# A list-scheduled two-layer encoder step: the planner's estimate lets a VectorE instruction between SBUF tiles last until the GpSimd product beside it ends

## The chip, the cores and the metric

The kernel runs on one core of a Trainium2 chip. The metric is the device time of one execution in microseconds (us), shown as the median of several runs. The engines are called as the profile calls them: PE is TensorE (PEld its weight load), DVE is VectorE, ACT is ScalarE, POOL is GpSimd, SP is SyncE, which here issues the DMAs.

## What is computed

Two layers of a hybrid encoder on 1104 tokens (64 of a running stream, 16 meta tokens and 1024 of a new one), width 1024. Each layer is, cut to what matters here:

```python
h = rmsnorm(x, norm_g)
z = h @ w_in                       # one projection, its columns split among the groups below
y_a = bg * conv(cg * xin) * silu(ga)                                   # short gated convolution
y_b = attention(rmsnorm(cq) @ w_uq, rmsnorm(ckv), kr) * silu(gb)       # 8 heads, latent keys, rotary part kr
zs = zc + (prev - zc) * shift_mu                                       # token shift
y_c = groupnorm(rwkv7_scan(r, decay, k, v, kk, a, s0)) * silu(gc)      # recurrence over tokens, 4 heads
x = x + concat([y_a, y_b, y_c]) @ w_out
```

A last RMSNorm follows, and the states of every group are outputs too.

## The kernel before

Features lie on the partitions, tokens along the free axis, in three groups of 336, 384 and 384 tokens (`GROUPS`). A projection of 128 output columns for one group (`project`) is 24 matmuls into one PSUM tile `prj`: 8 slices of the 1024 inputs, and for each `whi` by `hhi`, `whi` by `hlo` and `wlo` by `hhi`, since weights and activations are split into a high and a low half. ACT makes the high half and DVE the low one (`halves`: `whi`, then `wlo`). The weights' halves live in a ring of slots, so that a new `whi` waits until PE has finished with an older one.

The recurrence is done in chunks of 64 tokens. For each of 6 parts (3 token groups by 2 pairs of heads) `rwkv_prep` makes triangular matrices (PSUM tiles `x`, masked by DVE into `wq` or `wx`), transposes (`tm`), inverts 16 by 16 blocks on DVE with a chain of tiny instructions on 48 partitions (`tri`, `lora`) between two trips through DRAM (`dg`, `dt`), and combines blocks on PE (`inv`). `rwkv_scan` then carries the state from chunk to chunk: a product `xp`, an addition on DVE (`wr`), a copy on ACT (`wx`), a product `sp`, and the new `state` on DVE. `rwkv_finish` takes a product `yp`, the group norm, a transpose `ym` and the gate. GpSimd takes products between SBUF tiles: the token shift (`zd`), norm factors (`xin`, `krt`, `cq`, `ckv`) and gates (`gate`, `qa`).

The order of the instructions is made when the program is written. Every operation goes through `Meter`, which keeps for each engine a time at which it comes free, for each tile the times of its last writes and reads, and gives each instruction a cost from its engine, operation and size (`note`). The main stream (the projections, `inproj_rest`) issues its matmuls one by one; after each, `pump` looks at the side streams (prep, scan, finish, attention's preparation), asks with `due` when what their next step needs will be ready by the estimate, and lets a step go in between when that is no later than PE's clock and a margin. So the estimate decides how many projection matmuls stand between two steps of the recurrence. The engines themselves take their instructions in the order in which they were issued, and semaphores make them wait for data.

`place` can put an instruction into an earlier gap of its engine in the estimate:

```python
for i, (a, b) in enumerate(idle):
    s = max(a, t)
    if s + cost <= b:
        ...
        return s
s = max(t, self.free[eng])
```

All instructions stand on one line of the profile (line 82, the call through which every operation is recorded), so groups are told apart by their tiles.

Of the kernel before, what the change touches and what calls it, by code (L numbers as in the profile page):

```python
# [55 lines left out]
COLUMNS = (*(11 + m for m in MIXED), 18, 19, 0, 1, 2, KR, *range(3, 11), *range(20, 24))  # L56
NEVER = 1e9
LEAD = 0.0
WARM = 8
NEAR = 0.0  # L60
LAZY = -1.3
# [10 lines left out]
class Engine:  # L72


    def __init__(self, meter, name, eng):
        self.meter, self.name, self.eng = meter, name, eng
# [12 lines left out]
class Meter:  # L89


    def __init__(self, nc):
        self.nc = nc
        self.free = dict.fromkeys(("tensor", "vector", "scalar", "gpsimd", "sync"), 0.0)
        self.seen, self.rings, self.part = {}, {}, (128, 128)
        self.idle = {e: [] for e in self.free}
        for e in self.free:
            setattr(self, e, Engine(self, e, getattr(nc, e)))

# [30 lines left out]
    def note(self, eng, op, args, kw):  # L130
        aps = [x for x in args + tuple(kw.values()) if isinstance(x, bass.AP)]
        if not aps:
            return
        outs = [kw["out"] if "out" in kw else args[0]] + ([kw["accum_out"]] if "accum_out" in kw else [])
        ins = [x for x in aps if not any(x is o for o in outs)]
        size = lambda x: int(np.prod(x.shape[1:]))
        n = max(size(x) for x in outs[:1] + ins)
        if eng == "tensor":
            l, r = args[1], args[2]
            p, q = (2, 1) if op == "transpose" else (4, 2) if l.dtype == F32 else (1, 1)  # L140
            l, r = (r, l) if op == "transpose" else (l, r)
            cost, late = max(size(r) * p, 2 * size(l) * q) / 2320, 0.0
            if l.dtype == F32 and size(l) <= 64 and op == "matmul":
                cost = 0.02 + size(r) * 2 / 2320
            cost += 0.003
            up = lambda x: 32 if x <= 32 else 64 if x <= 64 else 128
            part = (up(l.shape[0]), up(size(l))) if l.dtype == F32 and op == "matmul" else (128, 128)
            cost += CHANGE if part != self.part else 0.0
            self.part = part
        elif op == "dma_start":  # L150
            cost, late = 0.45, 2.0 + size(outs[0]) * outs[0].shape[0] * 4 / 2e5
        else:
            fast = op in ("tensor_copy", "tensor_scalar") and all(x.space == bass.MemoryType.SB for x in aps)
            cost, late = {"vector": 0.1 + n * 0.54e-3 if fast else 0.1 + n * 1.06e-3, "scalar": (0.37 if "accum_out" in kw else 0.18) + n * 0.83e-3,
                          "gpsimd": 0.15 + n * (0.7e-3 if op == "memset" else 2.1e-3 if op == "tensor_tensor" else 3.4e-3)}[eng], 0.0
        t = self.place(eng, max([self.when(x, eng) for x in ins] + [self.when(x, eng, True) for x in outs]), cost)
        for x in ins:
            self.touch(x, eng, t + cost + late, False)
        for x in outs:
            self.touch(x, eng, t + cost + late, True)  # L160
# [35 lines left out]
class Net:  # L196
# [86 lines left out]
    def race(self, streams, fill):  # L283
# [3 lines left out]
        while run:  # L287
            more = fill if self.solo else []
            t, q = next(((0.0, q) for q in run + more if self.due(q[0]) <= self.clock + LEAD), (NEVER, None))
            if q is None:  # L290
# [1101 lines left out]
    def run(self):  # L1392
# [16 lines left out]
        ps = self.psp("warm")  # L1409
        for _ in range(WARM):  # L1410
            self.mm(ps[:, :128], self.ones, self.ones, start=True, stop=True)
# [168 lines left out]
```

## Time and profile before

| what | value |
|---|---|
| median of 3 runs | 1530.34 us (1526.41 to 1530.67) |
| the profiled execution | 1529.08 us, span of its instructions 1527.0 us |
| PE busy | 1463.1 us, 96% of the span |
| DVE busy | 1063.0 us, 70% |
| ACT busy | 772.1 us, 51% |
| POOL busy | 253.1 us, 17% |
| mean granted TensorE clock | 0.988 |

A row of a timeline gives an instruction's start and duration in us, its engine, operation, tiles written and read, shapes and count, and in brackets how long its engine had been idle before it and what ended that. Matmuls overlap in their records, so their pace is read from start to start. A table by windows gives each engine's busy time in a stretch and the granted TensorE clock there, where 1.00 is 2.4 GHz and 0.50 is 1.2 GHz.

### The profile page before, as it was taken

What the parts mean: (1) busy time and instruction counts of PE and PEld (TensorE: products, weight loads), DVE (VectorE), ACT (ScalarE), POOL (GpSimd) and SP (SyncE); (2) the same over time, 40 slices, a digit from 0 to 9 for tenths busy, and PEclk for the clock granted to TensorE, in tenths of its full rate; (3) what the DMA queues carried; (4) which work ended last, traced back from release to release, by engine and by line L of the source; (5) the groups of instructions that cost most, each with busy time, mean ns of one, the idle gap of its engine ahead of it and who ended that gap; (6) DMA issues with size and microseconds to landing.
All of it is one profiled execution on the core that took longest, in us unless ns stands there. A gap on an engine that the chain in (4) does not pass through costs nothing.

```text
span 1527.0 us, 30583 instructions
## 1 busy us (share of the span) xinstructions
PE 1463.1 (96%) x12076; PEld 1310.9 (86%) x12076; DVE 1063.0 (70%) x2477; ACT 772.1 (51%) x1846; POOL 253.1 (17%) x281
## 2 busy tenths in 40 slices
PE   8999999999999999999999999999999999999996
PEld 7989988999887878779999898898998768788795
DVE  7565687676778676575845666876767877686566
ACT  7125454444567575563522355445356775565442
POOL 0222212222121101000011222212122301111002
PEclk9999999999999999999999999999999999999998
DMA  6322212322225101122322312212322331012123
GB/s 209 137 83 81 68 50 57 88 55 75 82 86 164 31 26 39 55 74 63 141 103 99 117 33 60 88 30 81 76 67 77 129 98 47 24 35 85 41 66 119
DMA packets 95471, 119.81 MB, mean 78 GB/s; under 512 B 41889, under 2 KB 74785, under 8 KB 95329
## 3 DMA queue, kind: packets, MB, share of 16 engines
q1 hardware_dynamic: 95328, 117.87, 25.4%
q8 instruction: 95, 1.56, 0.4%
q14 instruction: 48, 0.39, 0.1%
HBM read 81.24 MB, written 36.60 MB: 77 GB/s over the span
## 4 chain that ended last, share of the span: by engine, by line
PE 51%; DVE 10%; ACT 5%; issue 3%; DMA 2%; POOL 1%; DVEq 0%; SPq 0%; ACTq 0%; POOLq 0%
PE prj L82 24%; PE sc L82 6%; PE po L82 6%; PE tr L82 5%; PE upq L82 3%; PE val L82 1%; PE inv L82 1%; DVE st L82 1%; DVE p L82 1%; PE upk L82 1%; ACT p L82 1%; DVE wq L82 1%; DVE out L82 1%; ACT pt L82 1%; ACT wq L82 1%
## 5 line engine op out<-in xcount | busy, mean ns | idle before, releaser
L82 PE MATMUL prj<-hhi,whi 128*128 128x384 f32 (+1 forms) x1152 | 392.0, 340 | 4.2 <-DVE z L82 2.6
L82 PE MATMUL prj<-hlo,whi 128*128 128x384 f32 (+1 forms) x1152 | 391.9, 340 | 0.1
L82 PE MATMUL prj<-hhi,wlo 128*128 128x384 f32 (+1 forms) x1152 | 391.1, 339 | 0.7 <-DVE wlo L82 0.7
L82 PEld LDWEIGHTS prj<-hhi,whi 128*128 128x128 f32 x1152 | 219.7, 191 | 7.5 <-issue 2.9
L82 PEld LDWEIGHTS prj<-hlo,whi 128*128 128x128 f32 x1152 | 219.6, 191 | 4.1 <-issue 0.9
L82 PEld LDWEIGHTS prj<-hhi,wlo 128*128 128x128 f32 x1152 | 219.5, 191 | 4.0 <-DVE wlo L82 1.0
L82 PE MATMUL prj<-yhi,wo 128*128 128x384 f32 (+2 forms) x776 | 206.5, 337 | 2.5 <-DVE xn L82 2.0
L82 PE MATMUL sc<-ka,qa 128*128 128x264 f32 (+9 forms) x720 | 156.3, 337 | 6.0 <-ACT p L82 2.5
L82 ACT ACTIVATE p<-sc,st 128x144 f32<-128x144 f32 (+8 forms) x240 | 127.9, 541 | 42.4 <-DVE st L82 41.6
L82 PEld LDWEIGHTS prj<-yhi,wo 128*128 128x128 f32 x776 | 138.6, 189 | 5.1 <-DVE xn L82 3.1
L82 DVE TENSOR_REDUCE st<-sc 128x1 f32<-128x512 f32 (+9 forms) x240 | 118.1, 501 | 23.9 <-PE sc L82 22.3
L82 PE MATMUL prj<-ylo,wo 128*128 128x384 f32 (+2 forms) x388 | 129.6, 334 | 0.0
L82 PEld LDWEIGHTS sc<-ka,qa 128*128 128x128 f32 (+1 forms) x720 | 112.3, 188 | 18.8 <-ACT p L82 6.4
L82 ACT ACTIVATE pt<-tr 128x512 f32<-128x512 f32 (+3 forms) x174 | 92.4, 546 | 70.2 <-PE tr L82 68.2
L82 PE MATMUL tr<-cst,p 128*128 128x128 f32 (+2 forms) x752 | 115.5, 277 | 4.5 <-ACT pt L82 3.1
L82 PEld LDWEIGHTS tr<-cst,p 128*128 128x128 f32 (+2 forms) x752 | 83.2, 141 | 28.3 <-issue 10.3
L82 POOL TENSOR_TENSOR qa<-qt,qa 128x512 fp32r<-128x512 f32 (+1 forms) x40 | 49.7, 1244 | 338.6 <-ACT qa L82 338.5
L82 ACT ACTIVATE whi<-wraw 128x1024 fp32r<-128x1024 f32 (+1 forms) x49 | 51.0, 1041 | 97.4 <-PE prj L82 82.5
L82 PE MATMUL po<-pt,v 128*64 128x256 f32 (+3 forms) x864 | 94.3, 354 | 0.4 <-ACT pt L82 0.4
L82 DVE TENSOR_SCALAR p<-p,st 80x336 f32<-80x336 f32 (+5 forms) x144 | 84.2, 587 | 1.8
L82 DVE TENSOR_TENSOR wlo<-wraw,whi 128x1024 fp32r<-128x1024 f32 (+1 forms) x49 | 71.4, 1458 | 16.9 <-ACT whi L82 16.8
L82 PEld LDWEIGHTS po<-pt,v 128*64 128x64 f32 (+1 forms) x864 | 53.2, 137 | 27.4 <-issue 4.5
(232 smaller groups left out, 2641.9 us busy)
## 6 DMA issues: line engine op xcount, KB each, us to landing
wraw<-w_in SPq DMA_DIRECT2D x47, 512.0 KB, 3.6
wraw<-w_out SPq DMA_DIRECT2D x32, 256.0 KB, 2.6
zd<-z SPq DMA_DIRECT2D x14, 576.0 KB, 3.5
wr<-zd SPq DMA_DIRECT2D x36, 192.0 KB, 2.8
gd<-gate SPq DMA_DIRECT2D x12, 552.0 KB, 3.4
yraw<-yd SPq DMA_DIRECT2D x8, 552.0 KB, 3.8
xn<-x SPq DMA_DIRECT2D x8, 552.0 KB, 4.2
xd<-xn SPq DMA_DIRECT2D x8, 552.0 KB, 2.9
```

What stands on the lines that cost most here:

```text
L82: r = f(*args, **kw)
```

## The change

The estimate of an instruction's cost changes; what is computed does not. `Meter` now remembers the stretches in which it has placed GpSimd products (`busy`). A DVE instruction of four kinds, all of whose operands lie in SBUF and which has at most 512 elements per partition, and which would begin at DVE's frontier while such a product runs, is given a cost that reaches 0.1 us past the product's end.

```diff
+SHARES = ("tensor_tensor", "scalar_tensor_tensor", "tensor_copy", "tensor_scalar")
...
-        self.idle = {e: [] for e in self.free}
+        self.idle, self.busy = {e: [] for e in self.free}, []
...
-        t = self.place(eng, max([self.when(x, eng) for x in ins] + [self.when(x, eng, True) for x in outs]), cost)
+        ready = max([self.when(x, eng) for x in ins] + [self.when(x, eng, True) for x in outs])
+        if eng == "vector" and op in SHARES and n <= 512 and all(x.space == bass.MemoryType.SB for x in aps):
+
+            t = max(ready, self.free[eng])
+            cost = max([cost] + [b - t + 0.1 for a, b in self.busy if a < t + 0.1 < b])
+        t = self.place(eng, ready, cost)
+        if eng == "gpsimd" and op == "tensor_tensor":
+            self.busy = self.busy[-40:] + [(t, t + cost)]
```

The instructions stay the same but for six copies out of PSUM, which move from ACT to DVE. Their order changes from the first part of the recurrence on. In the rows below L82 of the kernel before is L83 of the changed one.

**Place A**, PE's order in the first part of layer 1, where the triangular products `x` end and the transposes `tm` begin (`prj` are projection matmuls). Before:

```order
L82 MATMUL x_128_963<-wb_884,wx_886 64x128
L82 MATMUL x_129_964<-wb_884,wx_886 64x128
L82 MATMUL prj_939<-hhi_158,wlo_791 128x336
L82 MATMUL prj_989<-hhi_151,whi_790 128x384
L82 MATMUL prj_989<-hlo_159,whi_790 128x384
L82 MATMUL prj_989<-hhi_151,wlo_791 128x384
L82 MATMUL prj_989<-hhi_152,whi_790 128x384
L82 MATMUL tm_994<-cst,wx_886 128x128 x3
L82 MATMUL prj_989<-hlo_160,whi_790 128x384
L82 MATMUL tm_999<-cst,wx_886 128x128 x3
```

The same place in the changed kernel, the end of it:

```order
L83 MATMUL prj_989<-hlo_166,whi_790 128x384
L83 MATMUL prj_989<-hhi_158,wlo_791 128x384
L83 MATMUL prj_1015<-hhi_151,whi_790 128x384
L83 MATMUL prj_1015<-hlo_159,whi_790 128x384
L83 MATMUL prj_1015<-hhi_151,wlo_791 128x384
L83 MATMUL prj_1015<-hhi_152,whi_790 128x384
L83 MATMUL prj_1015<-hlo_160,whi_790 128x384
L83 MATMUL tm_1021<-cst,wx_886 128x128 x3
L83 MATMUL tm_1026<-cst,wx_886 128x128 x3
```

Between the last `x` and the first `tm` there stood 5 projection matmuls, and now there stand 30. Layer 2 has the same counts.

**Place B**, DVE's order in the third part of the recurrence, beside the rotary keys (`kr`, `krt`) and the projection `xin`. `wr<-xp` is the scan's addition, for which ACT's `wx` and then PE's `sp` wait; `wq<-dg` and `wa<-dt` are the inverted blocks, for which PE's `inv` waits; `wlo` is the low half of the next weights. Before:

```order
L82 COPY tri_2207<-tri_2207 48x256
L82 TENSOR_TENSOR kr_2305<-kr_2305 32x384
L82 SCALAR_TENSOR_TENSOR kr_2305<-krt_2306,rot 32x384
L82 TENSOR_TENSOR wlo_2394<-wraw_2303,whi_2393 128x1024
L82 SCALAR_TENSOR_TENSOR krt_2306<-krt_2306,rot 32x384
L82 TENSOR_TENSOR wr_1412<-xp_2425,wq_1423 64x128
...
L82 TENSOR_TENSOR kr_2305<-kr_2305 32x384
L82 SCALAR_TENSOR_TENSOR state_140<-sp_2473,dc_1483,sd_2423 64x64 x2
L82 TENSOR_TENSOR wq_2054<-dg_2204,cst 128x6x64
L82 TENSOR_TENSOR wa_2053<-dt_2286,cst 128x384
L82 TENSOR_TENSOR wlo_2497<-wraw_2397,whi_2496 128x1024
```

Now:

```order
L83 TENSOR_TENSOR wlo_2394<-wraw_2270,whi_2393 128x1024
L83 COPY tri_2207<-tri_2207 48x256
L83 TENSOR_TENSOR kr_2272<-kr_2272 32x384
L83 TENSOR_TENSOR wr_1435<-xp_2445,wq_1446 64x128
L83 COPY u_2391<-par_88 128x2
L83 MEMSET u_2391 128x2
L83 TENSOR_SCALAR lora_2728<-lora_2728 64x384
L83 TENSOR_TENSOR wlo_2492<-wraw_2397,whi_2491 128x1024
L83 TENSOR_TENSOR wq_2074<-dg_2204,cst 128x6x64
L83 TENSOR_TENSOR wa_2073<-dt_2327,cst 128x384
```

Two more instructions on `kr` now stand ahead of `wr<-xp` (all of the last `kr` group is done there), and the next `wlo` has moved from behind `wq<-dg` and `wa<-dt` to ahead of them. On PE at this place, 17 projection matmuls fewer stand between the products `cum` and `x`, 20 more between `x` and `sp`, and `inv` follows `sp` after 6 of them and 10 of 12 `x` of the next set, where there were 22 and none. On ACT the three `lora` instructions stand behind `wx` instead of ahead of it, and `whi` behind them. Layer 2 has the same order.

**Place C**, PE's order in the fourth part, between `yp` and `inv`, which needs DVE's masked `wx`. Before:

```order
L82 MATMUL x_394_3149<-wb_2792,wx_2794 64x128
L82 MATMUL yp_3163<-wr_2043,wq_2054 64x64 x12
L82 MATMUL inv_3186<-wq_2736,wa_2735 64x64 x12
L82 MATMUL inv_3199<-wa_2735,wq_2736 64x64 x12
L82 MATMUL prj_3113<-hlo_165,whi_2854 128x384
```

Now:

```order
L83 MATMUL yp_3190<-wr_2063,wq_2074 64x64 x12
L83 MATMUL prj_3157<-hlo_160,whi_3030 128x336
L83 MATMUL prj_3157<-hhi_152,wlo_3031 128x336
L83 MATMUL prj_3157<-hhi_153,whi_3030 128x336
L83 MATMUL prj_3157<-hlo_161,whi_3030 128x336
L83 MATMUL prj_3157<-hhi_153,wlo_3031 128x336
L83 MATMUL inv_3218<-wq_2745,wa_2744 64x64 x12
```

Five projection matmuls have come between, in both layers. In the sixth part the opposite happened: two that stood ahead of `yp` are gone.

## Rows read from the trace of the kernel before

**Rows 1.** The page's first part: busy time of each engine.
```profile
PE 1463.1 (96%) x12076; PEld 1310.9 (86%) x12076; DVE 1063.0 (70%) x2477; ACT 772.1 (51%) x1846; POOL 253.1 (17%) x281
```

**Rows 2.** Windows: length, busy PE, PEld, DVE, ACT, POOL; clock, DMA, GB/s.
```profile
98.00:102.00 4.00, 3.83 (x13) 3.12 (x14) 1.55 (x7) 1.42 (x4) 0.00 (x0) 0.57 0.92 239
232.00:236.00 4.00, 3.65 (x12) 3.65 (x13) 3.89 (x8) 2.12 (x5) 3.22 (x3) 0.50 0.87 193
236.00:240.00 4.00, 4.00 (x40) 3.79 (x42) 1.99 (x3) 1.51 (x3) 0.82 (x1) 0.69 0.01 2
```

**Rows 3.** Timeline of PE at place A, then layer 2's wait.
```profile
94.14 0.89 PE L82 MATMUL x<-wb,wx 64*64 64x128 f32 x24
...
95.75 0.33 PE L82 MATMUL prj<-hhi,whi 128*128 128x384 f32 x1
98.17 0.57 PE L82 MATMUL tm<-cst,wx 128*128 128x128 f32 x3 [2.09 <-ACT wa L82]
...
846.05 0.90 PE L82 MATMUL tm<-cst,wx 128*128 128x128 f32 x3 [2.01 <-ACT wa L82]
```

**Rows 4.** Timeline of DVE at place A.
```profile
95.61 0.15 DVE L82 TENSOR_SCALAR zd<-z 128x1 f32<-128x1 f32 x1 [1.94 <-POOL zd L82]
...
97.14 1.02 DVE L82 TENSOR_TENSOR wq<-x,cst 128x384 f32<-128x384 f32 x2
```

**Rows 5.** Timelines of DVE and PE: the inverted blocks behind place A.
```profile
105.50 0.56 DVE L82 TENSOR_TENSOR z<-prj,rs 128x384 f32<-128x384 f32 x1 [1.38 <-PE prj L82]
...
122.25 0.55 DVE L82 TENSOR_TENSOR wa<-dt,cst 128x384 f32<-128x384 f32 x1
...
123.82 0.85 PE L82 MATMUL inv<-wa 64*64 64x64 f32 x21
```

**Rows 6.** Timeline of PE at place B, then layer 2's wait.
```profile
222.80 0.34 PE L82 MATMUL prj<-hhi,whi 128*128 128x384 f32 x1
...
228.36 0.34 PE L82 MATMUL prj<-hhi,wlo 128*128 128x384 f32 x1
232.35 0.80 PE L82 MATMUL sp<-wr,wt 128*128 128x128 f32 x2 [3.65 <-ACT wx L82]
...
239.26 0.85 PE L82 MATMUL inv<-wa 64*64 64x64 f32 x21
...
980.41 0.80 PE L82 MATMUL sp<-wr,wt 128*128 128x128 f32 x2 [3.56 <-ACT wx L82]
```

**Rows 7.** Timelines of DVE and POOL at place B.
```profile
211.72 0.58 DVE L82 SCALAR_TENSOR_TENSOR state<-sp,dc,sd 64x64 f32<-64x64 f32 x2 [0.82 <-PE sp L82]
...
222.15 0.55 DVE L82 SCALAR_TENSOR_TENSOR kr<-krt,rot 32x384 f32<-32x384 f32 x1
...
228.11 1.15 DVE L82 SCALAR_TENSOR_TENSOR kr<-krt,rot 32x384 f32<-32x384 f32 x1
229.29 1.81 DVE L82 TENSOR_TENSOR wlo<-wraw,whi 128x1024 fp32r<-128x1024 f32 x1
...
231.71 0.28 DVE L82 TENSOR_TENSOR wr<-xp,wq 64x128 f32<-64x128 f32 x1
...
227.63 2.39 POOL L82 TENSOR_TENSOR xin<-xin,rs 128x336 f32<-128x336 f32 x2
```

**Rows 8.** Timeline of ACT around place B's wait.
```profile
228.54 1.63 ACT L82 ACTIVATE lora<-lora 64x384 f32<-64x384 f32 x3 [2.07 <-DMA lora<-zd]
...
237.66 1.06 ACT L82 ACTIVATE whi<-wraw 128x1024 fp32r<-128x1024 f32 x1 [1.59 <-PE prj L82]
```

**Rows 9.** Timeline of PE at place C.
```profile
295.31 0.92 PE L82 MATMUL inv<-wq,wa 64*64 64x64 f32 x24 [1.39 <-DVE wx L82]
```

**Rows 10.** DVE and POOL at 92 us, and POOL at 64 us.
```profile
92.40 1.22 DVE L82 TENSOR_TENSOR wlo<-wraw,whi 128x1024 fp32r<-128x1024 f32 x1
...
92.62 2.96 POOL L82 TENSOR_TENSOR zd<-z 128x1151 f32<-128x1151 f32 x1 [4.98 <-issue]
...
64.64 2.11 POOL L82 TENSOR_TENSOR zd<-z 128x1151 f32<-128x1151 f32 x1 [4.27 <-DVE z L82]
```

## The prediction

> **What bounds the kernel now.** I read the busy times first: PE is busy for 1463.1 of 1527.0 us, so no other engine is the bound, and a change of order can win at most PE's 63.9 us of idle time and what a lowered clock costs beside them [rows 1]. Then PE's timeline, for its waits over 2 us inside the projections, and the windows around them. Two places stand out, once in each layer. At place A PE waits 2.09 and 2.01 us ahead of the transposes `tm` [rows 3]. At place B it waits 3.65 and 3.56 us ahead of `sp` [rows 6]. Behind both the granted clock goes from 1.00 to 0.50, that is from 2.4 to 1.2 GHz: the mean of 98 to 102 us is 0.57, so 4 x 0.43 = 1.7 us of PE's work are lost there, and at 232 to 240 us 4 x 0.50 + 4 x 0.31 = 3.2 us [rows 2]. Place A costs 2.1 + 1.7 = 3.8 us a layer, place B 3.65 + 3.2 = 6.9 us.
>
> Last, DVE and POOL at these places, for why the estimate was wrong. At place B a 32x384 instruction on `kr` takes 0.55 us alone and 1.15 us beside a product on `xin`, and the `wlo` behind it 1.81 instead of 1.22 us [rows 7, 10]. DVE is held until the product ends, and what stands behind it, `wr` and then `sp`, is late. At place A DVE waits 1.94 us for the product `zd`, and only then masks `x` into `wq`, on which `tm` depends [rows 4]. The old estimate could put those masks into the gap; a copy that fills the gap in the estimate takes that away.
>
> **The change, part by part.** No instruction is added and none goes, so the holds themselves stay. What moves is what PE does while it would wait. Projection matmuls of 384 columns start (228.36 - 222.80)/32 = 0.174 us apart at full clock [rows 6].
>
> *Place A.* PE now has 30 projection matmuls between `x` and `tm` instead of 5: 30 x 0.174 = 5.2 us, so it comes to `tm` at some 100.2 us. `tm` was ready at 98.17, so the wait goes with 2 us to spare [rows 3]. That is worth 2.09 + 2.01 = 4.1 us, and 2 x 1.7 = 3.4 us more if the clock then stays up, 7.5 us in all. What is late next is `inv`: by the two orders PE does 146 instead of 135 projection matmuls between `x` and `inv`, 1.9 us more, and so reaches it at 123.82 - 3.8 + 1.9 = 121.9 us. The blocks were ready at 122.25 + 0.55 = 122.8 us; but the 1.38 us in which DVE waited for a `prj` in the middle of that chain go too, since that projection now ends earlier, which makes 121.4 [rows 5]. I take -7.5; the bounds are -7.5 and, with the clock falling elsewhere, -4.1.
>
> *Place B.* DVE works almost without a gap here, so its order sets the times. `wr` ended at 231.71 + 0.28 = 232.0 us. Two more instructions on `kr` ahead of it are 2 x 0.55 = 1.1 us, and DVE's 0.82 us of waiting earlier on go: 232.3, and `sp` some 0.35 later, as now, at 232.65 [rows 6, 7]. Behind it the new order is worse. ACT takes `wx` (0.3), three `lora` (1.63) and only then `whi` (1.06), to 235.3 us [rows 8]; DVE's `wlo` waits for that `whi` with 1.22 us [rows 10], and `wq` and `wa` now queue behind `wlo` with 0.55 each [rows 5]: `inv` can start at some 237.75. PE meanwhile has `sp` (0.25), 6 projections (1.0) and 10 of 12 `x` (0.89 x 10/12 = 0.75): it is there at 234.65 and waits 3.1 us. `inv` is thus 239.26 - 237.75 = 1.5 us earlier than now, but with 17 - 20 + 16 = 13 projections fewer done since `cum` (2.25 us) and 0.75 us of `x` more: -1.5 + 2.25 - 0.75 = 0 [rows 6]. The old wait is cut into pieces and the largest one moves to `inv`. A wait of that length is followed by the lower clock now, so 3.2 us a layer may come on top; since short products follow there and not projections, I take half of it, +1.6 a layer, +3.2 in all. The bounds are -6.9 a layer (wait and low clock both gone) and +3.2.
>
> *Place C and the sixth part.* Five matmuls of 336 columns, 5 x 0.15 = 0.8 us, 0.174 scaled by 336/384, now cover part of the 1.39 us wait ahead of `inv`, -1.6 in both layers [rows 9]. The two matmuls lost in the sixth part uncover at most 0.35 us a layer, +0.7.
>
> *The rest.* Every later step moves by some matmuls, in attention too. The named places hold 14.1 of the 63.9 us of idle time; the other 50 us are made of many short waits, which I let stand as they are, with 3 us to either side.
>
> The sum: -7.5 + 3.2 - 1.6 + 0.7 = -5.2 us on the profiled execution's 1529.08 us, or **1524 us**. That execution lies 1.3 us below the median of 1530.34. About 0.3%, 4.6 us, is what a measurement of this kernel can tell from no change; 1524 is 0.4% below the median, so close to that line.
>
> **The rivals.**
>
> *Place B's wait goes altogether.* If `lora` and `whi` land earlier than I chain them, the later `sp` and the earlier `kr` leave no long wait: -7.5 - 13.8 - 0.9 = -22 us, 1507 us. For it speaks that 20 more projections stand between `x` and `sp`; against it, that 17 of them were taken from ahead of `x`.
>
> *The gain of place A is given back.* If DVE's chain of tiny instructions doesn't move up, PE waits 0.9 us more at each `inv` behind place A, and place C stays bound by GpSimd's product. Then -7.5 + 1.8 + 3.2 + 0.7 = -1.8 us, 1527 us, not to be told from no change.
>
> *The hold works the other way too.* The product `zd` takes 2.11 us beside a waiting DVE and 2.96 us where it began just behind a `wlo` that was running, and that `wlo` ran in its plain 1.22 us [rows 10]. So whichever comes first goes through, and the estimate, which only lengthens DVE's instructions, would place products up to 0.85 us too early and hold DVE where it isn't held. Two late products a layer at places A and C would eat 4 x 0.85 = 3.4 of the 5.2 us: 1527 us. The Trainium skill ("SBUF — State Buffer", section "SBUF: two separate sides") states this as a lock on a port pair that VectorE and GpSimd share, taken by whichever starts first for its whole instruction, while the other fully blocks; by that rule the estimate stays wrong on GpSimd's side, and the rows named agree with it.
>
> *Slower: `inv` behind `wlo`, at place B.* If `wlo` is held as it is now (1.81, +0.6) and `wq` like `kr` (1.15, +0.6) [rows 7], the wait ahead of `inv` grows from 3.1 to 4.3 us, and with the clock low for as long behind it as now that is 1.2 + 3.2 = 4.4 us a layer, +8.8. With place A giving back its waits alone (-4.1) and the sixth part's 0.7, the sum is +5.4 us: 1534.5 us. It decides from a loss at place B that is over 8 us greater than now's 13.8, or over 12 us where place A gives its full 7.5. For it speaks that DVE is the engine that is full here, and that the order puts a wait for ACT ahead of what PE needs.
>
> *The change does not do what it says.* Excluded by the order: PE's instructions differ from the first part of the recurrence on.
>
> **How the numbers follow.** The forecast, places A to C as summed, has 0.42 and gives 1517 to 1531 by its bounds. Place B without a wait has 0.10, place A given back 0.20, the hold the other way 0.08, slower 0.20. Faster by over 0.3% (below 1525.7) is the forecast and the first rival, 0.52; within 0.3% the next two, 0.28; slower 0.20. The range takes in most of the slow case and half of the fast one: 1508 to 1535 us.
>
> **What would show it.** In the profile of the changed kernel: at about 98 us `tm` starts with no wait named and the granted clock of that stretch is 1.00, in both layers; near 205 to 240 us a wait of some 3 us stands ahead of `inv`, ended by DVE `wa`, instead of one ahead of `sp`, and PE's busy time stays near 1463 us with idle time near 59. The step for place A is wrong if a wait over 1 us stands ahead of `tm` or of the `inv` behind it; the one for place B if `sp` still waits over 2 us or `inv` under 1 us. The whole is wrong if new waits of 2 us or more show in attention, which I let stand.

## The result, and the profile after

The changed kernel takes 1553.28 us (median of 4 executions, 1553.08 to 1553.82) against 1530.51 us of the kernel before beside it: 1.0155 times as long, 95% interval 1.0136 to 1.0174. That is slower, and outside the predicted range.

| | before | after |
|---|---|---|
| span of the profiled execution | 1527.0 us | 1551.3 us |
| PE busy | 1463.1 us | 1473.2 us |
| PE idle (span less busy) | 63.9 us | 78.1 us |
| mean granted clock | 0.988 | 0.980 |
| span x (1 - clock) | 18.3 us | 31.0 us |

Of the 24.3 us, 14.2 are new idle time of PE and 10.1 are PE busy longer, with more time at the lower clock (12.7 us by the last line). Executions of one and the same kernel differ by up to 10 us here, along with their mean granted clock (1553.28 us at 0.974 and 1543.45 us at 0.982 in one of the runs below), so times are read from medians and places from waits. The page's first part, against [rows 1]:

```profile
PE 1473.2 (95%) x12076; PEld 1320.0 (85%) x12076; DVE 1066.7 (69%) x2483; ACT 768.4 (50%) x1840; POOL 262.2 (17%) x281
```

DVE and ACT are busy for as long as before within 4 us, POOL for 9 us more; PE has the same number of matmuls, so this is a matter of order. Place A came out as forecast in the main. PE's timeline there, against [rows 3], with layer 2's wait as its last row, and DVE's, against [rows 4]:

```profile
99.94 0.82 PE L83 MATMUL tm<-cst,wx 128*128 128x128 f32 x6
...
104.56 0.55 PE L83 MATMUL tm<-cst,wb 128*128 128x128 f32 x3 [1.07 <-DVE wx L83]
...
122.58 0.62 PE L83 MATMUL inv<-wa 64*64 64x64 f32 x14
...
866.05 0.55 PE L83 MATMUL tm<-cst,wb 128*128 128x128 f32 x3 [1.47 <-DVE wx L83]
```

```profile
95.28 0.15 DVE L83 TENSOR_SCALAR zd<-z 128x1 f32<-128x1 f32 x1 [1.93 <-POOL zd L83]
```

DVE waits for GpSimd's product as before, but PE is busy with 30 projection matmuls meanwhile and meets the first `tm` without a wait; a new, smaller wait of 1.07 us, 1.47 us in layer 2, comes ahead of the last transposes of the group. The windows, against [rows 2], show the clock:

```profile
98.00:102.00 4.00, 4.00 (x26) 3.78 (x25) 1.79 (x6) 1.06 (x3) 0.00 (x0) 1.00 0.51 168
...
181.00:185.00 4.00, 3.21 (x51) 3.10 (x52) 0.34 (x1) 2.02 (x5) 0.00 (x0) 0.57 0.01 4
...
244.00:248.00 4.00, 4.00 (x64) 3.31 (x64) 1.22 (x3) 0.89 (x2) 0.00 (x0) 0.50 0.01 5
```

It stays at 1.00 (2.4 GHz) at 98 us, where it was 0.57, but falls to 0.57 and to 0.50 at places that PE's timeline names. These are PE's waits behind place A in layer 1 that the text below speaks of, then the two longest of layer 2, which repeats them. Those at 236 and 303 us are not new: they were 3.65 and 1.39 us [rows 6, 9].

```profile
181.79 1.54 PE L83 MATMUL inv<-wq,wa 64*64 64x64 f32 x24 [3.96 <-ACT wa L83]
...
235.97 0.80 PE L83 MATMUL sp<-wr,wt 128*128 128x128 f32 x2 [1.57 <-ACT wx L83]
...
243.76 1.23 PE L83 MATMUL inv<-wa 64*64 64x64 f32 x18 [4.13 <-DVE wa L83]
...
303.05 0.91 PE L83 MATMUL inv<-wq,wa 64*64 64x64 f32 x24 [1.25 <-ACT wa L83]
...
306.08 0.92 PE L83 MATMUL inv<-wa,wq 64*64 64x64 f32 x24 [2.12 <-DVE wx L83]
...
333.19 0.46 PE L83 MATMUL xp<-state,wb 128*128 128x128 f32 x2 [1.92 <-DVE state L83]
...
367.65 0.92 PE L83 MATMUL inv<-wq,wa 64*64 64x64 f32 x24 [1.88 <-DVE wx L83]
...
944.20 1.54 PE L83 MATMUL inv<-wq,wa 64*64 64x64 f32 x24 [4.29 <-ACT wa L83]
...
1007.18 1.23 PE L83 MATMUL inv<-wa 64*64 64x64 f32 x18 [4.79 <-DVE wa L83]
```

In the kernel before, the `inv` that now waits 3.96 us had this wait:

```profile
179.10 0.91 PE L82 MATMUL inv<-wq,wa 64*64 64x64 f32 x24 [1.06 <-DVE wx L82]
```

Counting projection matmuls tells where the time goes: the changed kernel starts the 703rd 5.8 us earlier than the one before (154.0 instead of 159.8 us), the 1171st 5.3 us later, and leaves layer 1's projections 10.6 us behind. In attention it stays 10 to 13 us behind. Layer 2 does the same again: 5.5 us behind at the 3150th, past its place A, 27.9 us at the 3978th, 24.5 at the end. The loss lies in the projections, between places A and the end of the recurrence, and none in attention.

Behind the new waits stand instructions that are long or wait for something else, ahead of a short one that PE needs. At 181.8 us it is in ACT's queue (first fence: after; second: before):

```profile
180.30 1.06 ACT L83 ACTIVATE whi<-wraw 128x1024 fp32r<-128x1024 f32 x1 [4.12 <-DMA wraw<-w_in]
181.26 0.47 ACT L83 ACTIVATE wa<-inv 128x384 f32<-128x384 f32 x1
```

```profile
177.68 0.47 ACT L82 ACTIVATE wa<-inv 128x384 f32<-128x384 f32 x1
180.70 1.06 ACT L82 ACTIVATE whi<-wraw 128x1024 fp32r<-128x1024 f32 x1 [2.54 <-DMA wraw<-w_in]
```

`whi`, the high half of weights that PE does not need yet, waits 4.12 us for its transfer, and the copy `wa<-inv`, whose product PE ended before 177 us, stands behind it. In the kernel before the two stood the other way round. The same on DVE, at 301, 331 and 366 us:

```profile
301.22 1.22 DVE L83 TENSOR_TENSOR wlo<-wraw,whi 128x1024 fp32r<-128x1024 f32 x1
302.35 0.55 DVE L83 TENSOR_TENSOR wx<-x,cst 128x384 f32<-128x384 f32 x1
304.44 0.56 DVE L83 TENSOR_TENSOR cv<-cv,xin 128x384 f32<-128x384 f32 x1 [1.54 <-POOL xin L83]
...
305.38 0.55 DVE L83 TENSOR_TENSOR wx<-x,cst 128x384 f32<-128x384 f32 x1
...
331.01 1.72 DVE L83 TENSOR_TENSOR wlo<-wraw,whi 128x1024 fp32r<-128x1024 f32 x1
332.76 0.29 DVE L83 SCALAR_TENSOR_TENSOR state<-sp,dc,sd 64x64 f32<-64x64 f32 x1
...
366.53 0.51 DVE L83 TENSOR_TENSOR cv<-cv,xin 128x336 f32<-128x336 f32 x1 [2.55 <-POOL xin L83]
366.96 1.01 DVE L83 TENSOR_TENSOR wx<-x,cst 128x384 f32<-128x384 f32 x2
```

A `wlo` and a product that waits for GpSimd lie between and ahead of the masks `wx`, and a `wlo` parts the two halves of `state`.

One sentence ahead of the prediction has to be put right: an engine's queue does not hold the instructions in the order in which the program wrote them. The numbers in the tiles' names count up as the program takes tiles; in ACT's queue of the changed kernel `whi` with 2266 stands ahead of a copy of `inv` with 1841:

```
L83 ACTIVATE ckv_192_1520<-prj_227_1814 128x336
L83 ACTIVATE whi_293_2266<-wraw_226_1812 128x1024
L83 ACTIVATE wa_175_1445<-inv_228_1841 128x384
```

So the language reorders instructions between the program and the queues, and here it put forward a `whi` whose transfer had not yet landed on the chip. `Meter`'s order is only what it starts from.

### The profile page after: what moved, and what is told of

Its sections match the earlier page's. It is cut to its first block, busy times and chain, and to the rows that moved or that the text cites. A ratio compares the mean times of both kernels' runs of the same rounds, so it can differ in the third digit from the quotient of the medians.

```text
span 1551.3 us, 30562 instructions
## 1 busy us (share of the span) xinstructions
PE 1473.2 (95%) x12076; PEld 1320.0 (85%) x12076; DVE 1066.7 (69%) x2483; ACT 768.4 (50%) x1840; POOL 262.2 (17%) x281
## 4 chain that ended last, share of the span: by engine, by line
PE 68%; DVE 17%; ACT 6%; DMA 4%; issue 3%; POOL 1%; SPq 0%; DVEq 0%; ACTq 0%; POOLq 0%
PE prj L83 36%; PE sc L83 6%; PE po L83 6%; PE tr L83 5%; PE upq L83 3%; PE inv L83 3%; DVE lora L83 2%; DVE wq L83 2%; DVE tri L83 1%; DVE wlo L83 1%; PE val L83 1%; PE w L83 1%; PE upk L83 1%; DVE p L83 1%; DMA wraw<-w_in 1%
## 5 line engine op out<-in xcount | busy, mean ns | idle before, releaser
L83 PE MATMUL prj<-hhi,whi 128*128 128x384 f32 (+1 forms) x1152 | 393.6, 342 | 3.3 <-DVE z L83 2.4
L83 PE MATMUL prj<-hhi,wlo 128*128 128x384 f32 (+1 forms) x1152 | 392.1, 340 | 1.9 <-DVE wlo L83 1.9
L83 PE MATMUL prj<-hlo,whi 128*128 128x384 f32 (+1 forms) x1152 | 393.6, 342 | 0.1
L83 PEld LDWEIGHTS prj<-hhi,whi 128*128 128x128 f32 x1152 | 220.8, 192 | 7.6 <-issue 2.9
L83 PEld LDWEIGHTS prj<-hhi,wlo 128*128 128x128 f32 x1152 | 220.5, 191 | 5.4 <-DVE wlo L83 2.4
L83 PEld LDWEIGHTS prj<-hlo,whi 128*128 128x128 f32 x1152 | 220.4, 191 | 4.1 <-DVE hlo L83 0.8
L83 PE MATMUL prj<-yhi,wo 128*128 128x384 f32 (+2 forms) x776 | 208.6, 338 | 3.0 <-DVE xn L83 2.0
L83 PE MATMUL sc<-ka,qa 128*128 128x144 f32 (+8 forms) x720 | 157.5, 337 | 7.1 <-ACT p L83 2.3
L83 ACT ACTIVATE p<-sc,st 128x144 f32<-128x144 f32 (+8 forms) x240 | 128.0, 542 | 41.3 <-DVE st L83 40.8
L83 PEld LDWEIGHTS prj<-yhi,wo 128*128 128x128 f32 x776 | 138.6, 188 | 6.5 <-DVE xn L83 3.8
L83 DVE TENSOR_REDUCE st<-sc 128x1 f32<-128x512 f32 (+8 forms) x240 | 118.1, 503 | 28.1 <-PE sc L83 25.6
L83 PE MATMUL prj<-ylo,wo 128*128 128x384 f32 (+2 forms) x388 | 130.1, 335 | 0.0
L83 PEld LDWEIGHTS sc<-ka,qa 128*128 128x128 f32 (+1 forms) x720 | 113.2, 188 | 19.6 <-ACT p L83 6.9
L83 ACT ACTIVATE pt<-tr 128x512 f32<-128x512 f32 (+3 forms) x172 | 90.7, 544 | 78.3 <-PE tr L83 76.5
L83 PE MATMUL tr<-cst,p 128*128 128x128 f32 (+2 forms) x752 | 115.7, 276 | 1.0 <-DVE st L83 0.3
L83 POOL TENSOR_TENSOR qa<-qt,qa 128x512 fp32r<-128x512 f32 (+1 forms) x40 | 49.7, 1244 | 337.4 <-ACT qa L83 337.4
L83 PEld LDWEIGHTS tr<-cst,p 128*128 128x128 f32 (+2 forms) x752 | 84.1, 141 | 24.0 <-issue 11.9
L83 PE MATMUL po<-pt,v 128*64 128x256 f32 (+3 forms) x864 | 96.0, 356 | 0.0
L83 ACT ACTIVATE whi<-wraw 128x1024 fp32r<-128x1024 f32 (+1 forms) x49 | 50.9, 1039 | 84.8 <-PE prj L83 64.3
L83 DVE TENSOR_SCALAR p<-p,st 80x336 f32<-80x336 f32 (+5 forms) x144 | 84.1, 586 | 1.6
L83 DVE TENSOR_TENSOR wlo<-wraw,whi 128x1024 fp32r<-128x1024 f32 (+1 forms) x49 | 69.6, 1421 | 15.4 <-ACT whi L83 15.3
L83 PEld LDWEIGHTS po<-pt,v 128*64 128x64 f32 (+1 forms) x864 | 53.9, 137 | 26.7 <-issue 5.1
```

Of the source, the lines that this page charges most:

```text
L83: r = f(*args, **kw)
```

## The experiments

Theories: **Q**, the loss is made by what stands ahead in the queues, at places that come about when the lengthened estimate moves the steps of the recurrence against the columns of the projections; **H**, DVE is held longer beside GpSimd (comparing each DVE instruction beside a product with the median of its form without one gives 78 holds and 58.7 us before, 88 and 67.1 after); **W**, some of the lengthened instructions are wrongly lengthened and cost the time; **G**, what is won at one place is given back at the next. The estimate lengthens 36 instructions in all: the one-element `zd` beside the four token shifts (seven in all, by 2.1 to 2.6 us each) and 29 others (by 0.01 to 0.83 us); the expectations of `zd_only` and `no_zd` say 8 and 28.

**One place alone: `whi_behind`.** `issue_after` is the language's call that keeps what the block issues behind an instruction of the same engine.

```diff
-        nc.scalar.activation(Pm, o, AF.Copy)
+        self.first = nc.scalar.activation(Pm, o, AF.Copy)
...
+                if m == COLUMNS[13]:
+                    with self.tc.issue_after(self.first.ins):
+                        self.halves(hi, lo, t)
```

> The changed kernel, with one edit: in each layer the high half `whi` of the weights of the first `xin` column is kept behind `wa<-inv` in ACT's queue; the orders of PE, DVE and SP stay the same. Theory Q (the lengthened estimate moves the steps of the recurrence so that long instructions which wait for something else stand just ahead of short ones that PE needs, and PE waits there): the wait ahead of `inv` at 181.8 us falls from 3.96 us to under 1 us and at 944 us from 4.29 us likewise, the low clock behind it goes, and the kernel is 6 to 10 us faster than the changed one, 1543 to 1547 us. Rival H (the loss is that DVE is held longer beside GpSimd: 67.1 instead of 58.7 us): nothing changes, 1553 us within 2. Rival G (given back: PE takes what it gains as a wait at the next column, whose weights come no earlier): 1550 to 1553 us with a new wait of 2 us or more ahead of the first `prj` of that column.

Measured: 1547.8 us (1543.45 to 1553.28), 1.0096 [1.0073, 1.0119] of before, where the changed kernel has 1.0155 and, beside later runs, 1.0167: 0.6 to 0.7% less, 9 us or more. In its trace, ACT and then PE:

```profile
179.19 0.47 ACT L83 ACTIVATE wa<-inv 128x384 f32<-128x384 f32 x1
```

```profile
179.71 0.92 PE L83 MATMUL inv<-wq,wa 64*64 64x64 f32 x24 [0.35 <-ACT wa L83]
```

Two instructions exchanged in each layer take the wait from 3.96 to 0.35 us. This speaks for Q at this place and against H. A part is given back, as G says: the trace is of the slowest execution, 1553.28 us, and in it PE's idle time falls by 3.6 us alone (74.5 against 78.1), with 4.93 us in each layer ahead of place B's `inv` instead of 4.13 and 4.79.

**The change in two parts, and another shift.** `zd_only` lengthens only the one-element `zd`, `no_zd` only the others; `before_dve11` is the kernel before with a slightly dearer DVE.

```diff
 zd_only
-        if eng == "vector" and op in SHARES and n <= 512 and all(...):
+        if eng == "vector" and op in SHARES and n == 1 and op == "tensor_tensor" and all(...):
 no_zd
+        if eng == "vector" and op in SHARES and 1 < n <= 512 and all(...):
 before_dve11
-            cost, late = {"vector": 0.1 + n * 0.54e-3 if fast else 0.1 + n * 1.06e-3, ...
+            cost, late = {"vector": 0.11 + n * 0.54e-3 if fast else 0.11 + n * 1.06e-3, ...
```

> The changed kernel with the lengthening kept only for the one-element `zd` instructions beside the four token shifts of a layer, 8 of the 36 that the estimate lengthens in all; PE's order is that of the changed kernel up to the second part of the recurrence, and in layer 2 that of the kernel before from the fifth part on. Theory Q: place A's gain of 6 to 7 us a layer stays; what follows has waits of its own, which I can't tell beforehand in layer 1, and in layer 2 no more than a few us; 1515 to 1540 us. Rival W (the other 28 lengthened instructions are wrongly lengthened, and they alone cost the time): place A's gain is all that is left, 1530.5 - 13 = 1517 us within 3. Rival H: as many holds as in the changed kernel where it is slow, fewer where it is fast.

> The changed kernel with the lengthening left out for the one-element `zd` instructions and kept for the other 28; PE's order is that of the kernel before up to the second part, so place A keeps its waits of 2.09 and 2.01 us. Rival W (the 28 bear the loss): 1553 + 13 = 1566 us within 4. Theory Q (it is where the steps land and not which instructions are lengthened): anything from 1530 to 1560 us, with other places that wait than in the changed kernel.

> The kernel before, with the estimate's fixed cost of a DVE instruction 0.11 instead of 0.10 us and nothing else; this shifts the steps of the recurrence by 16 projection matmuls on average, the change of this study by 15. Theory Q in its strong form (any shift of this size leaves the places which the old order had been fitted to): slower than before by 5 us or more, 1535 to 1560 us, with waits of 2 to 4 us at new places. Rivals W and H (what the lengthening says, or the holds, are the cause): within 5 us of the kernel before, 1526 to 1535 us.

Measured, as ratios to before: `zd_only` 1.0021 [1.0008, 1.0034], `no_zd` 1.0008 [0.9994, 1.0022], `before_dve11` 1.0070 [1.0045, 1.0095]. The two parts of the change cost 0.2 and 0.1% and together 1.55%: neither part bears the loss by itself, which ends W. H falls too: `zd_only` has more held time (92 holds, 69.5 us) than the changed kernel and is 20 us faster. A change of 10 ns per DVE instruction that means nothing costs 0.7%, as Q expects. Each order has long waits of its own; the longest of `zd_only`, at place B's `inv` again, then of `no_zd`, at an `inv` of the fifth part:

```profile
239.93 1.33 PE L83 MATMUL inv<-wa 64*64 64x64 f32 x20 [4.31 <-ACT xin L83]
```

```profile
360.75 1.54 PE L83 MATMUL inv<-wq,wa 64*64 64x64 f32 x24 [6.01 <-DVE wx L83]
```

**Place B.** The transfers there, in the changed kernel: SP's queue, `dg`'s landing, and DVE.

```profile
235.21 0.38 SPq L83 DMA_DIRECT2D wraw<-w_in  x1
...
236.68 0.37 SPq L83 DMA_DIRECT2D dg<-tri  x1
...
DMA to landing us min/median/max: 4.3/4.3/4.3
...
239.94 1.23 DVE L83 TENSOR_TENSOR wlo<-wraw,whi 128x1024 fp32r<-128x1024 f32 x1 [1.77 <-ACT whi L83]
241.09 1.35 DVE L83 TENSOR_TENSOR wq<-dg,cst 128x384 f32<-128x384 f32 x1
242.36 1.34 DVE L83 TENSOR_TENSOR wa<-dt,cst 128x384 f32<-128x384 f32 x1
```

`dg` lands at 236.7 + 4.3 = 241.0 us, just when `wq` starts, so that `wlo` ahead of it may cost nothing. For these runs and the next ones `behind` notes the work in the estimate at its old place and issues it behind a named instruction, so that PE's order stays the same but for a few matmuls (16 in `fix_b`, 50 in `fix_6`). The line that records every operation is L84 or L85 in these kernels.

```diff
+    def behind(self, site, work, after=None):
+        if site not in BEHIND:
...
+        self.nc.plan = True
+        work()
+        self.nc.plan = False
+
+        def emit(ins=None):
+            self.nc.mute = True
...
+                with self.tc.issue_after(ins.ins):
+                    work()
+            self.nc.mute = False
...
+        if i == 2:
+            self.came(("col", 15), r)
```

`fix_b` puts `wlo` behind the masks, `fix_b2` the weight load behind `dg` and `dt` as well, `fix_b3` the loads of `wr` too. `after_again` is the changed kernel beside them.

> The changed kernel itself, beside the next three on the same chip: 1553 us within 3.

> The changed kernel, with one edit at place B of each layer: `wlo` is kept behind the masks `wq<-dg` and `wa<-dt` in DVE's queue; PE's order stays the same. Theory Q1 (`inv` waits for `wa` because `wlo`, which waits 1.77 us for ACT, stands ahead of both masks): the wait ahead of `inv` falls from 4.13 and 4.79 us to under 2 us, and the kernel is 6 to 10 us faster than the changed one, 1543 to 1547 us. Rival D (the masks can't start earlier: `dg` was issued at 236.7 us behind the 512 KB weight load of 235.2 us and took 4.3 us to land, where it takes 2.0 elsewhere, so that it lands at 241.0, just when `wq` starts): the wait of `inv` stays within 1 us of what it was, 1551 to 1555 us.

> The edit of the run before, and the weight load ahead of `dg` and `dt` in SP's queue at place B put behind them. Rival D: `dg` and `dt` land in 2 to 3 us instead of 4.3 and 4.1, the masks start some 2 us earlier, the wait ahead of `inv` falls by 2 us or more in each layer, 1542 to 1549 us. Theory Q1 gives the same as the run before, as the load would change nothing. If the three loads of `wr`, 192 KB each, which now stand ahead of `dg`, take the place of the weight load, the landing stays at 4 us and the time at 1553 us.

> The changed kernel with place B alone put in order: `wlo` behind the masks, and both the weight load and the three loads of `wr` behind `dg` and `dt`. By D: `dg` lands in 2 to 2.5 us, `inv` waits 2 us less than in the changed kernel in each layer, and 1546 to 1551 us. Without a gain at the landing: 1553 us within 2, as with the two runs that moved `wlo` and the weight load.

Measured: `after_again` 1555.36 us, 1.0167 [1.0149, 1.0184]; `fix_b` 1552.8, 1.0147 [1.0130, 1.0164]; `fix_b2` 1555.58, 1.0174 [1.0155, 1.0192]; `fix_b3` 1554.64, 1.0154 [1.0139, 1.0169]. None can be told from the changed kernel. In `fix_b` the first mask waits for `dg`, in `fix_b3`, with neither the weight load nor the loads of `wr` ahead of it, it lands sooner:

```profile
242.14 0.77 DVE L85 TENSOR_TENSOR wq<-dg,cst 128x384 f32<-128x384 f32 x1 [2.79 <-DMA dg<-tri]
```

```profile
239.49 0.38 SPq L85 DMA_DIRECT2D dg<-tri  x1
...
DMA to landing us min/median/max: 2.3/2.3/2.3
...
241.79 0.60 DVE L85 TENSOR_TENSOR wq<-dg,cst 128x384 f32<-128x384 f32 x1 [0.80 <-DMA dg<-tri]
```

So D (the masks wait for the landing of `dg`) is right on what they wait for, and Q1 (they wait for `wlo`) is wrong at this place. But D's times are wrong too: the 2 us gained at the landing came to 1.0 us in front of `inv` (3.12 us; 3.16 in layer 2, where it was 4.79) and to nothing that the time shows. Where the rest went was not found.

**All places of a layer.** `fix_6` is to put all six in order. It leaves out one product `cv<-cv,xin` of a token group in layer 1 (11 in its trace instead of 12; the expectation of `fix_6b` says in each layer); `fix_6b` does that product too. `fix_7` adds the loads of `wr`, `fix_late` has only the three later places.

```diff
 fix_6, fix_6b
+BEHIND = (('col', 13), ('col', 15), ('col', 18), ('col', 19), ('mask', 3), ('mask', 4), ('load', 15))
 fix_7
+BEHIND = (('col', 13), ('col', 15), ('col', 18), ('col', 19), ('mask', 3), ('mask', 4), ('load', 15), ('wr', 3))
 fix_late
+BEHIND = (('col', 18), ('col', 19), ('mask', 3), ('mask', 4))
```

> The changed kernel with all six places of each layer put in order, PE's order the same but for some 50 matmuls at place B: `whi` behind `wa<-inv` (181.8 us), place B as in the run before, `wlo` behind the masks `wx` (302 us), `wlo` behind the second `state` instruction (331 us), and the products `cv<-cv,xin` behind the masks `wx` (304 and 366 us). Theory Q (waits made by what stands ahead in the queues are the loss): 3.6 + 2.5 + 1.5 + 1.9 + 1.7 = 11 us a layer of idle time go, of which a third comes back at the next dependence, with some 5 us of low clock: about 20 us faster than the changed kernel, 1528 to 1540 us. Rival H (longer holds beside GpSimd are the loss): within 3 us of 1553. Rival G (given back at the next wait): 1545 us or more.

> The six places of a layer in order, as in the run fix_6, which left out the product `cv<-cv,xin` of one group in each layer; here it is done, behind the masks `wx` like the others. Theory Q: 1533 us as there, plus what the product costs on DVE at worst, 2 x 0.56 us: 1532 to 1537 us. If the time there came from the work left out (in each layer 0.56 us and a wait of some 1.5 us for GpSimd, 4 us in all), 1537 to 1540 us. Rival H: 1553 us.

> The run before, and the three loads of `wr`, 192 KB each, behind `dg` and `dt` in SP's queue at place B too, so that neither they nor the weight load share the DMA engines with `dg`. Rival D of place B: `dg` lands in 2 to 2.5 us instead of 3.7, the wait ahead of `inv` at 238.5 us falls from 2.74 to 1.5 us or less, in layer 2 from 3.59 to 2.3, some 2 us and part of 5 us of low clock in all: 1528 to 1532 us. If the landing does not depend on what else is on its way: no change, 1533 us within 2.

> The changed kernel with only the three later places of a layer put in order (`wlo` behind the masks `wx` at 302 us and behind the second `state` instruction at 331 us, the products `cv<-cv,xin` behind the masks at 304 and 366 us), without `whi` behind `wa<-inv` and without place B. If the places add up: 7 us from `whi` alone, nothing from place B, so these bring 10 to 12 of the 18 us that all six brought: 1542 to 1546 us. If the gain of all six came from their order together, under 5 us: 1549 us or more.

Measured: `fix_6` 1533.46 us, 1.0028 [1.0016, 1.0039]; `fix_6b` 1536.39 us, 1.0037 [1.0023, 1.0050]; `fix_7` 1536.22 us, 1.0031 [1.0018, 1.0045]; `fix_late` 1548.54 us, 1.0114 [1.0097, 1.0132]. With PE's order that of the changed kernel but for some 50 matmuls, 1.2 of its 1.55 to 1.67% are gone, 18 us or more; in `fix_6b` PE's idle time is 1534.4 - 1470.5 = 63.9 us, what it was before. Its holds hardly move (90, 65 us). This is Q's main evidence. By the ratios `whi` carries 0.6 to 0.7%, place B nothing and the later places 0.4 to 0.5%, so that the parts nearly add up, though `fix_late` brings less than the 10 us expected of it. The loads of `wr` bring nothing (`dg` still takes 2.8 us). PE's timeline of `fix_6b`, where the changed kernel waited 4.13, 2.12 and 1.92 us:

```profile
237.23 1.22 PE L85 MATMUL inv<-wa 64*64 64x64 f32 x18 [3.81 <-DVE wa L85]
...
299.86 1.55 PE L85 MATMUL inv<-wa,wq 64*64 64x64 f32 x24 [2.18 <-DVE wx L85]
...
326.24 0.46 PE L85 MATMUL xp<-state,wb 128*128 128x128 f32 x2 [0.28 <-DVE state L85]
```

The second place is not cured: `wlo` went behind the masks `wx`, but the product `cv<-cv,xin` stayed between them and still waits 2.5 to 2.7 us for GpSimd, in all four kernels of this group.

**The same at place B of the kernel before.** `before_b14` has `wlo` behind `wr<-xp` there.

```diff
+BEHIND = (('col', 14),)
...
+                self.came(("col", 14), r, False)
```

> The kernel before, with one edit at its place B: `wlo` (1.81 us, held beside GpSimd) is kept behind the addition `wr<-xp` in DVE's queue, on which ACT's `wx` and PE's `sp` wait; PE's order stays the same. Theory Q: the wait ahead of `sp` falls from 3.65 and 3.56 us to 1.8 us, 3.6 us in all and up to 3 us of low clock: 1523 to 1527 us, faster than both kernels. Rival G (given back: `inv` behind it, which PE now reaches just as its blocks are ready, waits as much longer): 1530 us within 2, with a wait of 1.5 us or more ahead of `inv` at 237 us.

Measured: 1530.57 us, 1.0002 [0.9990, 1.0014]. The wait ahead of `sp` falls to 1.11 us and comes back ahead of `inv`; PE, then DVE:

```profile
228.97 0.49 PE L84 MATMUL sp<-wr,wt 128*128 128x128 f32 x2 [1.11 <-ACT wx L84]
...
237.25 1.43 PE L84 MATMUL inv<-wa 64*64 64x64 f32 x21 [4.09 <-DVE wa L84]
```

```profile
236.17 0.56 DVE L84 TENSOR_TENSOR wq<-dg,cst 128x384 f32<-128x384 f32 x1 [2.40 <-DMA dg<-tri]
```

G holds here: the masks wait for `dg`, the last trip of the chain through DRAM, and the edit only moved PE's wait. That this chain bounds place B was not shown by a run that shortens it.

**The size of the lengthening.** `plus0` and `plus42` change the 0.1 us by which it reaches past the product.

```diff
 plus0
+            cost = max([cost] + [b - t for a, b in self.busy if a < t + 0.1 < b])
 plus42
+            cost = max([cost] + [b - t + 0.4 for a, b in self.busy if a < t + 0.1 < b])
```

> The changed kernel, with the lengthened instruction ending with GpSimd's product in the estimate, and not 0.1 us behind it. PE's order is the changed kernel's up to the third part, then it departs by 8 to 12 projection matmuls. Theory Q: the places that wait are others from 200 us on, so that the time lies somewhere between 1530 and 1560 us and differs from the changed kernel's by 5 us or more. If lengthening as such costs the time, 1553 us within 4.

> The changed kernel, with the lengthened instruction ending 0.4 us behind GpSimd's product in the estimate, as held instructions end in the trace (at 226.5 us the product `xin` ends at 227.67 and the held `lora` behind it at 228.58 us). If the loss came from a lengthening that was still too short, this is nearer to the chip and so faster than the changed kernel by 5 us or more, with place A's gain kept: 1525 to 1545 us. Theory Q: another order, another set of waits, and no better for being nearer: 1530 to 1565 us.

Measured: 1538.3 us, 1.0050 [1.0034, 1.0066], and 1557.37 us, 1.0177 [1.0156, 1.0198]. With 0, 0.1 and 0.4 us the same idea costs 0.5, 1.55 and 1.8%. The one that ends as held instructions do in the trace is no better, and its longest wait is that of `sp` at place B:

```profile
235.80 0.79 PE L83 MATMUL sp<-wr,wt 128*128 128x128 f32 x2 [6.29 <-ACT wx L83]
```

**A version faster than both: `nozd_cv`.** The wait of 6.01 us of `no_zd` stands behind two products, as DVE's timeline of `no_zd` shows:

```profile
355.83 0.51 DVE L83 TENSOR_TENSOR cv<-cv,xin 128x336 f32<-128x336 f32 x1 [2.55 <-POOL xin L83]
...
359.58 0.56 DVE L83 TENSOR_TENSOR cv<-cv,xin 128x384 f32<-128x384 f32 x1 [2.77 <-POOL xin L83]
360.05 1.01 DVE L83 TENSOR_TENSOR wx<-x,cst 128x384 f32<-128x384 f32 x2
```

```diff
+CV = {(1, 0): 4, (1, 1): 4}
+BEHIND = (('mask', 4),)
```

> The run no_zd with one edit in each layer: its two products `cv<-cv,xin` at 356 and 360 us (1103 and 1107 us), which wait 2.55 and 2.77 us for GpSimd, are put behind the two masks `wx` in DVE's queue, for which `inv` waits 6.01 and 4.83 us there. Theory Q: both waits fall under 1.5 us and the 6.8 us of low clock behind each go in part: 8 to 9 us of idle time and 2 to 6 us of clock, 1518 to 1524 us, faster than the kernel before and the changed one. Rival G (given back at the next dependence): 1530 us within 3, with a wait of 2 us or more within 20 us behind the place.

Measured: 1522.73 us (1519.99 to 1525.77), 0.9948 [0.9929, 0.9968] of before, 2% less than the changed kernel. In layer 1 the wait falls from 6.01 to 1.89 us, not quite to the 1.5 us expected; in layer 2 from 4.83 to 0.93. PE's timeline:

```profile
356.32 0.91 PE L85 MATMUL inv<-wq,wa 64*64 64x64 f32 x24 [1.89 <-ACT wa L85]
```

## Why the prediction was wrong

*Place A: right in the main.* The first `tm` starts without a wait at 99.94 us (forecast 100.2), the clock there is 1.00, and the `inv` behind it starts at 122.58 us with 11 more projection matmuls done. That is 123.82 - 122.58 + 1.9 = 3.1 us gained in layer 1 of the 3.75 put down for it. By the prediction's own sign, a wait over 1 us ahead of `tm`, the step is wrong in a small part: the last three `tm`, which it did not look at, wait 1.07 and 1.47 us. The rival that gives the gain back was wrong.

*Place B: the kind was right, the size and the reason were not.* A wait ended by `wa` stands ahead of `inv`, as forecast, but 4.13 and 4.79 us instead of 3.1, and `sp` keeps 1.57 us that I had at none. I chained `whi`, `wlo` and the masks, and left out the transfers: `dg` lands at 241.0 us, and the masks, held beside `xin`, take 1.35 us each instead of 0.55. `sp` itself starts at 235.97 us, 3.3 us later than summed. Idle time there is 4.13 + 1.57 + 0.97 (ahead of a `prj` that waits for `wlo`) against 3.65, 3 us more in layer 1, and the clock is low for 10.2 us instead of 6.8 in each layer. The slower rival named this place with the right sign and the wrong mechanism: `fix_b` took `wlo` away and nothing changed.

*Place C: wrong.* The forecast was -1.6 us. The wait ahead of the first `inv` stays at 1.25 us, against 1.39 [rows 9], and a new one of 2.12 us comes ahead of the second, behind `wlo` and `cv<-cv,xin`, in both layers. The sixth part is near its forecast of +0.7 us: the wait ahead of its `inv` is 1.26 us where 0.76 had been.

*The rest: the step that failed.* "Every later step moves by some matmuls ... which I let stand as they are, with 3 us to either side." Outside the named places the idle time did not stand: 181.8 us took 3.96 us where 1.06 had been, and 333 and 368 us took 1.92 and 1.88 us, with the like in layer 2, most with a stretch of lower clock behind it. How far the changed kernel falls behind between equal counts of projection matmuls (440, 640, 870, 1110, 1260 and 1620 of a layer's 1776) gives each place its share, in us of both layers together: some -7 at place A (forecast -7.5), +12 in the second part of the recurrence (nothing), +8 at place B (+3.2), +8 at place C (-1.6), +9 from there to the end of the recurrence (+0.7) and -5 behind it. So more than half of the miss lies at the steps that were let stand, and the rest at places B and C. Reordering a few instructions, with PE's order kept but for some 50 matmuls, brings three quarters of the loss back (`fix_6b`); that shows the cause of this part. The sign I had given as the mark of this failure, new waits in attention, did not come; they came in the projections.

*The reason behind it.* I took a lengthened estimate for a better one and so for a better order. `plus0`, `plus42` and `before_dve11` show that the time does not follow the estimate's nearness to the chip: six shifted orders without further edits gave 1.0008 to 1.0177 times the old time, none faster. In the old order only places A and B had waits over 1.5 us in a layer's projections once the recurrence had begun; a shift of some 15 matmuls drew all the others anew, and each of the six orders has some of 1.5 to 6.3 us among them. Which of the 36 lengthened instructions moves which step was not tried. `fix_6b` is still 6 us above before, though place A's gain is in it: its idle time is the old one, its clock 0.981 instead of 0.988, and the wait at 299.9 us with low clock behind it is left; that this is all of it was not shown. In the prediction's numbers one does not follow: by its own bounds the forecast's lower end is 1507 us, as in the first rival, and not 1517.

## What to carry to other kernels

Where an order is made by an estimate, a change of the estimate redraws every place, and the old order's good places count as much as its two bad ones: read the new order at all of them for a long instruction that waits for a transfer or another engine ahead of a short one that the bound engine needs, before pricing the named places. Cure a bad wait where it stands, by holding the one instruction back behind the one that matters; two such instructions a layer were worth 0.6% (`no_zd` to `nozd_cv`), no rule tried in the cost model made a faster order here. Before curing, ask what the wait is ended by next: at place B the edits of the queues moved or shortened the wait, and none that was made there alone changed the time.

## What was not expected of the hardware

A transfer of 48 KB, `dg`, took 4.3 us to land when it was issued 1.5 us behind a 512 KB weight load and a load of 192 KB, and 2.3 us in `fix_b3`, where these loads stood behind it; how long so small a transfer takes depended here on what else SP had issued.

GpSimd and DVE held each other in turn in one stretch of the changed kernel, by the lengths of their instructions (DVE, then POOL):

```profile
109.23 1.21 DVE L83 TENSOR_TENSOR wlo<-wraw,whi 128x1024 fp32r<-128x1024 f32 x1
110.36 2.29 DVE L83 COPY tri<-tri 48x256 f32<-48x256 f32 x1
```

```profile
108.79 3.62 POOL L83 TENSOR_TENSOR zd<-z 128x1151 f32<-128x1151 f32 x1 [6.21 <-issue]
```

The product took 3.62 us where 2.11 is its time beside a waiting DVE [rows 10], `wlo` its plain 1.21, and the copy behind `wlo`, 0.36 us alone, ended 0.2 us behind the product. An estimate that lengthens DVE alone has only half of this. The Trainium skill ("SBUF — State Buffer", section "SBUF: two separate sides") says that the two engines share a pair of ports, which the one that starts first keeps for its whole instruction while the other is blocked. The durations here agree with it, 2.11 + 1.21 = 3.3 of the 3.62 us; the recorded starts do not, as the product is put down as starting 0.44 us ahead of the `wlo` that held it. No run shows that it costs time.
